# Sixteen rows of a grouped store, issued between the two halves of the last w2 load of an expert MLP

## The chip, the cores and the metric

The kernel runs on one core of one Trainium2 chip. The metric is the device time of one execution in microseconds. The times given are the median of several runs; the profile is of one execution, with its own time.

## The reference: what is computed

Eight experts, each with 256 rows of 512 numbers, go through two matrix products of their own with a ReLU between them. All inputs and the output are float32.

```
h   = max(matmul(x, w1) + b1, 0)       # x 8x256x512, w1 8x512x2048
out = matmul(h, w2) + b2               # w2 8x2048x512, out 8x256x512
```

The weights are 4 MB each, w1 and w2 for every expert: 64 MB of the 71.39 MB that the profile counts as read from HBM. The output is 4.19 MB.

## The kernel before

**Tiling.** TensorE works in float16. The weights come in by DMA on GpSimd's queue, which turns float32 into float16 on the way, so that a w1 or a w2 (4 MB in HBM) is 2 MB in SBUF. For one expert, `first_product` makes the hidden values in 16 pieces of 128 (each of four matmuls over the 512 inputs); ScalarE adds b1, applies ReLU and writes hT. `second_product` adds up b2 (one matmul with a row of ones) and 16 matmuls for each of two blocks of 128 output rows, in two PSUM tiles, po0 and po1. VectorE copies the one (L156) and ScalarE the other (L157) to an SBUF tile, from where it is stored.

**Staging.** The main loop (L229) runs over steps s = 0 to 10: step s holds the first product of expert s and the second product of expert s - 3 (LAG is 3). In steps 8, 9 and 10 only second products are left, of experts 5, 6 and 7. There are three buffers for w1 and three for w2.

**The ring.** The loads and some stores are issued on one queue, GpSimd's (POOL), in an order that the list `ring` fixes (L217 to L227): each entry has the step from which it is due, a function and its arguments, and at each step the loop takes entries from the head as long as they are due. An entry that isn't due holds up those behind it. `ordered` keeps the issue order of a queue as it stands in the program. A DMA that must wait (for a buffer to be free, or for the values that it stores) holds the queue. Entries at the end of the list: w2 of expert 6, w2 of expert 7, the store of experts 0 to 3, the store of experts 4 and 5.

**Halves.** The w2 of experts 6 and 7 is loaded as two DMAs of 1 MB in SBUF (`HALVED`, L91 to L93), and the second product of these experts first takes what reads the first half, for both output blocks, and then what reads the second (L175 to L178).

**Stores.** The results of experts 0 to 3 are gathered in one SBUF tile of 128 rows: expert e has rows 32e to 32e + 31, and each row holds eight output rows of 512 float32, 16 KB. They are stored together, 2 MB, by `flush` (L138 to L140) on GpSimd's queue. Experts 4 and 5 are gathered likewise, 64 rows each with 8 KB in a row, 1 MB. The tiles of experts 6 and 7 have 4 KB in each of 128 rows and are stored at once (L164): that of expert 6 in three parts (`PARTS`, L40), rows 0 to 24 and 121 to 127 by SyncE's queue and rows 25 to 120 by ScalarE's; that of expert 7 in one part by SyncE's queue.

Of the kernel before, what the change touches and what calls it, by code (L numbers as in the profile page):

```python
# [10 lines left out]
def kernel(  # L11
# [9 lines left out]
    nc = tc.nc  # L21
    fp32 = mybir.dt.float32
    fp16 = mybir.dt.float16
    E, T, H = x.shape
    M = w1.shape[2]
    P = 128
    nTB = T // P
    nKC = H // P
    nJ = M // P
    B = 32  # L30
    nB = P // B
    LAG = 3
# [6 lines left out]

    PARTS = {E - 2: ((0, 25, False), (25, 121, True), (121, 128, False))}  # L40
    nXF32 = 2
    X_LOADS = {2: 2, 4: 4}

    def ordered(ins):
        return tc.keep_in_program_order(ins)
# [3 lines left out]
    w2_pool = ctx.enter_context(tc.tile_pool(name="w2", bufs=3))  # L49
# [16 lines left out]
    w2_sb = [None] * E  # L66
    hT = [None] * E
    pending = {}
# [16 lines left out]
            out=w1_sb[e], in_=w1[e].rearrange("(p kc) m -> p kc m", kc=nKC)  # L85
        ))

    def load_w2(e):
        src = w2[e].rearrange("(p j) h -> p j h", j=nJ)
        w2_sb[e] = w2_pool.tile([P, nJ, H], fp16, tag="w2", name="w2sb")  # L90
        half = nJ // 2 if e in HALVED else nJ  # L91
        for lo in range(0, nJ, half):
            ordered(nc.gpsimd.dma_start(out=w2_sb[e][:, lo : lo + half], in_=src[:, lo : lo + half]))  # L93

    def transposes(e):
# [39 lines left out]
            if j == nJ // 2 and e + 1 < E:  # L135
                transposes(e + 1)

    def flush(first):  # L138
        dst, src = pending.pop(first)
        ordered(nc.gpsimd.dma_start(out=dst, in_=src))  # L140

    def store(e, po):
        if e in group_of:
# [48 lines left out]
    for e in range(nXF32):  # L192
# [4 lines left out]
        out=b2_sb,  # L197
        in_=b2.rearrange("e h -> (e h)").rearrange("(o f) -> o f", o=1),
# [10 lines left out]
    for b in range(nB):  # L209
        nc.vector.transpose(  # L210
            out=b1T[b * B : (b + 1) * B, nB - 1 - b : nB - 1 - b + nJ * B],
            in_=b1_rows.rearrange("r (i j) -> r j i", j=nJ),
# [4 lines left out]
    ring = []  # L217
    for s in range(1, E + LAG - 1):
        if s < E:
            if s in X_LOADS:  # L220
                ring.append((s - 2, load_x, (s, X_LOADS[s])))
            ring.append((s - 2, load_w1, (s,)))
        if s >= LAG:
            ring.append((s - 2, load_w2, (s - LAG,)))
    ring.append((E + LAG - 3, load_w2, (E - 1,)))
    for first, n in GROUPS.items():
        ring.append((first + n + LAG, flush, (first,)))  # L227

    for s in range(E + LAG):  # L229
        while ring and ring[0][0] <= s:  # L230
# [37 lines left out]
```

## Time and profile before

| what | value |
|---|---|
| median of 3 runs | 181.62 us (181.58 to 181.81) |
| time of the profiled execution | 181.49 us |
| its span, first to last instruction | 179.7 us |
| TensorE matmul busy | 130.7 us, 73% of the span |
| VectorE, ScalarE busy | 87.4 us, 71.0 us |
| GpSimd's DMA queue | 3200 packets, 38.28 MB |
| SyncE's, ScalarE's DMA queue | 1.70 MB, 0.46 MB |
| granted TensorE clock, mean | 0.919 of full speed |

How to read it: "span" runs from the first to the last instruction in the profile, and the execution's own time is a little more. The busy time of TensorE is a sum over matmuls that overlap. A DMA is cut into packets, which sixteen DMA engines carry; the queue of an issuing engine has its own stream on each of them. The DMA share of a stretch is the mean busy share of the sixteen engines (a little over 1 is possible, since packets overlap slightly), and GB/s counts bytes as they are written, so a weight load counts half of what it reads. [...]

### The profile page before, as it was taken

What the parts mean: (1) busy time and instruction counts of PE and PEld (TensorE: products, weight loads), DVE (VectorE), ACT (ScalarE), POOL (GpSimd) and SP (SyncE); (2) the same over time, 40 slices, a digit from 0 to 9 for tenths busy, and PEclk for the clock granted to TensorE, in tenths of its full rate; (3) what the DMA queues carried; (4) which work ended last, traced back from release to release, by engine and by line L of the source; (5) the groups of instructions that cost most, each with busy time, mean ns of one, the idle gap of its engine ahead of it and who ended that gap; (6) DMA issues with size and microseconds to landing.
All of it is one profiled execution on the core that took longest, in us unless ns stands there. A gap on an engine that the chain in (4) does not pass through costs nothing.

```text
span 179.7 us, 1958 instructions
## 1 busy us (share of the span) xinstructions
PE 130.7 (73%) x784; PEld 87.4 (49%) x784; DVE 87.4 (49%) x125; ACT 71.0 (40%) x152; POOL 12.5 (7%) x27
## 2 busy tenths in 40 slices
PE   0005999159895970999769994959499986999960
PEld 0004899149793320794359543934189432434420
DVE  0999938990000199999998699203200020301010
ACT  3001699318793022491267406930559020020010
POOL 6000030200201010001100001000200021010000
PEclk9999999858999696599988999999969997899998
DMA  5999999999998999999999999999999999999995
GB/s 208 274 197 213 233 204 208 230 224 193 228 233 184 224 233 219 193 230 230 193 219 233 212 197 233 230 193 219 233 208 201 233 212 202 217 215 213 344 422 239
DMA packets 3844, 40.56 MB, mean 226 GB/s; under 512 B 460, under 2 KB 476, under 8 KB 1148
## 3 DMA queue, kind: packets, MB, share of 16 engines
q0 software_dynamic: 3200, 38.28, 96.4%
q1 hardware_dynamic: 476, 1.70, 2.5%
q10 hardware_dynamic: 160, 0.46, 0.6%
q8 instruction: 6, 0.10, 0.2%
q14 instruction: 2, 0.02, 0.0%
HBM read 71.39 MB, written 4.19 MB: 421 GB/s over the span
## 4 chain that ended last, share of the span: by engine, by line
DMA 67%; PE 27%; POOL 1%; issue 1%; ACT 0%; another core or an unknown queue 0%; POOLq 0%
DMA w1sb<-in_w_dram 44%; DMA w2sb<-in_w_dram 23%; PE po L178 17%; PE ph L121 10%; PE po L171 1%; POOL w1sb L84 1%; ACT out L157 0%; POOL b_sb L196 0%; POOL x L76 0%; POOLq L252 0%
## 5 line engine op out<-in xcount | busy, mean ns | idle before, releaser
L121 PE MATMUL ph<-xT,w1sb 128*128 128x256 f16 x512 | 66.7, 299 | 36.2 <-DMA w1sb<-in_w_dram 30.0
L121 PEld LDWEIGHTS <-w1sb 128*128 128x128 f16 x512 | 60.9, 148 | 42.7 <-DMA w1sb<-in_w_dram 38.6
L128 ACT ACTIVATE hT<-ph,b1T 128x256 f16<-128x256 f32 x128 | 56.7, 475 | 36.9 <-PE ph L121 22.1
L112 DVE STREAM_TRANSPOSE xT<-x 32x256 f16<-32x256 f16 (+1 forms) x64 | 52.7, 885 | 28.0 <-DMA x<-in_x_dram 22.0
L178 PE MATMUL po<-w2sb,hT 128*128 128x512 f16 x256 | 59.9, 395 | 6.6 <-DMA w2sb<-in_w_dram 6.5
L178 PEld LDWEIGHTS <-hT 128*128 128x128 f16 x256 | 25.7, 101 | 40.7 <-issue 14.4
L156 DVE COPY out<-po 32x512 f32<-32x512 f32 (+2 forms) x22 | 15.1, 688 | 52.5 <-PE po L178 52.2
L157 ACT COPY out<-po 32x512 f32<-32x512 f32 (+2 forms) x22 | 12.7, 578 | 65.5 <-PE po L178 65.3
L109 DVE STREAM_TRANSPOSE xT<-x 32x256 f16<-32x256 f16 x32 | 14.0, 436 | 0.5
L93 POOL DMA_DIRECT2D w2sb<-in_w_dram x10 | 5.3, 535 | 73.9 <-PE po L178 73.9
L84 POOL DMA_DIRECT2D w1sb<-in_w_dram x8 | 4.5, 559 | 62.7 <-PE ph L121 61.9
L171 PE MATMUL po<-b_sb,ones 1*128 1x512 f16 x16 | 4.8, 379 | 0.0
L210 DVE STREAM_TRANSPOSE b1T<-b_rows 32x512 f32<-32x512 f32 x4 | 4.1, 1028 | 0.0
L203 DVE CAST x<-x 128x1024 f16<-128x1024 f32 x2 | 1.4, 694 | 3.3 <-DMA x<-in_x_dram 3.3
L171 PEld LDWEIGHTS <-ones 1*128 1x128 f16 x16 | 0.9, 92 | 2.1 <-issue 2.1
L140 POOL DMA_DIRECT2D out_dram<-out x2 | 1.1, 540 | 11.1 <-ACT out L157 11.1
L189 ACT ACT_TABLE_LOAD x1 | 1.3, 1283 | 0.7 <-PEq L252 0.7
L76 POOL DMA_DIRECT2D x<-in_x_dram x2 | 1.1, 557 | 0.0
L188 DVE MEMSET ones<- 1x128 f16 x1 | 0.2, 165 | 0.8 <-PEq L252 0.8
L196 POOL DMA_DIRECT2D b_sb<-in_b_dram x1 | 0.5, 507 | 0.0
L189 ACT ACTIVATE warm<-ones 1x128 f16<-1x128 f16 x1 | 0.3, 308 | 0.0
L252 POOL MEMSET const-float32-0.0<- 128x1 f32 x1 | 0.1, 98 | 0.2 <-issue 0.2
(3 smaller groups left out, 0.3 us busy)
## 6 DMA issues: line engine op xcount, KB each, us to landing
w1sb<-in_w_dram POOLq DMA_DIRECT2D x8, 2048.0 KB, 37.0
w2sb<-in_w_dram POOLq DMA_DIRECT2D x6, 2048.0 KB, 49.7
w2sb<-in_w_dram POOLq DMA_DIRECT2D x4, 1024.0 KB, 24.0
out_dram<-out POOLq DMA_DIRECT2D x1, 2048.0 KB, 26.7
x<-in_x_dram SPq DMA_DIRECT2D x2, 512.0 KB, 4.0
x<-in_x_dram POOLq DMA_DIRECT2D x1, 1024.0 KB, 35.6
out_dram<-out POOLq DMA_DIRECT2D x1, 1024.0 KB, 17.7
x<-in_x_dram POOLq DMA_DIRECT2D x1, 512.0 KB, 24.5
```

The lines of the kernel that those rows point to most:

```text
L84: ordered(nc.gpsimd.dma_start(out=w1_sb[e], in_=w1[e].rearrange("(p kc) m -> p kc m", kc=nKC)))
L93: ordered(nc.gpsimd.dma_start(out=w2_sb[e][:, lo : lo + half], in_=src[:, lo : lo + half]))
L109: nc.vector.transpose(out=out[:, :, g, :, 0, :], in_=block[:, :, :, 0, :])
L112: nc.vector.transpose(out=out[:, tb, g], in_=block[:, tb])
L121: ordered(nc.tensor.matmul(out=ph, lhsT=w1_sb[e][:, kc, :].rearrange("p (q j) -> p q j", j=nJ)[:, :, j], rhs=xT[e][:, kc, :], start=(kc == 0),
L128: nc.scalar.activation(out=hT[e][:, j, :].rearrange("p (tb k i) -> p tb k i", tb=nTB, k=split), in_=ph.rearrange("p (tb i k) -> p tb k i", ...
L156: nc.vector.tensor_copy(out=out_sb[at : at + rows, k * nTB, :], in_=po[0][part])
L157: nc.scalar.copy(out=out_sb[at : at + rows, k * nTB + 1, :], in_=po[1][part])
L171: ordered(nc.tensor.matmul(out=t, lhsT=ones1, rhs=b2_sb[0:1, e * H : (e + 1) * H], start=True, stop=False,))
L178: ordered(nc.tensor.matmul(out=po[tb], lhsT=hT[e][:, j, tb * P : (tb + 1) * P], rhs=w2_sb[e][:, j, :], start=False, stop=(j == nJ - 1),))
L189: ordered(nc.scalar.activation(out=warm, in_=ones1, func=mybir.ActivationFunctionType.Relu))
L210: nc.vector.transpose(out=b1T[b * B : (b + 1) * B, nB - 1 - b : nB - 1 - b + nJ * B], in_=b1_rows.rearrange("r (i j) -> r j i", j=nJ),)
```

## The change

In the last entry pair of the ring, the first 16 of the 128 rows of the grouped store of experts 0 to 3 (256 KB of 2 MB) are issued between the first and the second half of the load of expert 7's w2. The other 112 rows are stored where all 128 were. For this `load_w2` takes a list of the parts that it issues, and `flush` a range of rows; the store keeps its entry until its last row is issued.

```diff
+    EARLY = 16
...
-    def load_w2(e):
+    def load_w2(e, parts=(0, 1)):
         src = w2[e].rearrange("(p j) h -> p j h", j=nJ)
-        w2_sb[e] = w2_pool.tile([P, nJ, H], fp16, tag="w2", name="w2sb")
+        if 0 in parts:
+            w2_sb[e] = w2_pool.tile([P, nJ, H], fp16, tag="w2", name="w2sb")
         half = nJ // 2 if e in HALVED else nJ
         for lo in range(0, nJ, half):
+            if lo // half not in parts:
+                continue
             ordered(nc.gpsimd.dma_start(out=w2_sb[e][:, lo : lo + half], in_=src[:, lo : lo + half]))
...
-    def flush(first):
-        dst, src = pending.pop(first)
-        ordered(nc.gpsimd.dma_start(out=dst, in_=src))
+    def flush(first, p0=0, p1=P):
+        dst, src = pending[first]
+        ordered(nc.gpsimd.dma_start(out=dst[p0:p1], in_=src[p0:p1]))
+        if p1 == P:
+            del pending[first]
...
-    ring.append((E + LAG - 3, load_w2, (E - 1,)))
+    ring.append((E + LAG - 3, load_w2, (E - 1, (0,))))
+    ring.append((E + LAG - 3, flush, (0, 0, EARLY)))
+    ring.append((E + LAG - 3, load_w2, (E - 1, (1,))))
     for first, n in GROUPS.items():
-        ring.append((first + n + LAG, flush, (first,)))
+        ring.append((first + n + LAG, flush, (first, EARLY if first == 0 else 0)))
```

GpSimd issues one DMA more than before. The instructions of the other engines, and the DMAs of SyncE's and ScalarE's queues, are the same and in the same order.

## The prediction

> **What bounds the kernel now.** I read four views, in this order: the forty slices of the page, the chain that ended last, the stretches of the tail, and the group of instructions that touch w2sb in the tail.
>
> The slices come first, because the page's chain gives 67% to DMA.
>
> ```profile
> PE   0005999159895970999769994959499986999960
> ...
> DMA  5999999999998999999999999999999999999995
> GB/s 208 274 197 213 233 204 208 230 224 193 228 233 184 224 233 219 193 230 230 193 219 233 212 197 233 230 193 219 233 208 201 233 212 202 217 215 213 344 422 239
> ```
>
> The sixteen DMA engines never rest between the first slice and the last; TensorE rests often. The rate doubles in the last three slices, and not because the engines work harder: a weight is read as four bytes and written as two, a result is written as four. So the end is the sum of the DMA work, unless the tail has a hole in it. The chain of waits says something else about the tail:
>
> ```profile
> 108.47 41.12 DMA w2sb<-in_w_dram
> 149.59 0.04 issue
> 149.63 8.75 PE po L178 x32
> 158.39 0.53 PE po L171 x2
> 158.92 7.01 PE po L178 x32
> 165.93 0.53 PE po L171 x2
> 166.47 7.03 PE po L178 x32
> 173.49 0.02 issue
> 173.52 0.59 ACT out L157
> ```
>
> By it, three second products run back to back after the w2 of expert 5 lands, then the copy, then (not in the chain) the store of expert 7. Two things might therefore set the end: these products, or the queues. The stretches decide:
>
> ```profile
> core 0: us, PE busy (x) PEld busy (x) DVE busy (x) ACT busy (x) POOL busy (x), PEclk, DMA share, GB/s
> 149.60:159.30 9.70, 9.66 (x37) 3.74 (x37) 1.38 (x2) 0.86 (x2) 0.00 (x0) 0.82 1.04 216
> 159.30:167.40 8.10, 8.10 (x38) 3.45 (x37) 0.69 (x1) 0.88 (x2) 0.54 (x1) 1.00 1.03 212
> 167.40:175.00 7.60, 6.08 (x29) 2.55 (x26) 0.69 (x1) 0.59 (x1) 0.00 (x0) 1.00 0.99 407
> 175.00:177.60 2.60, 0.00 (x0) 0.00 (x0) 0.00 (x0) 0.00 (x0) 0.00 (x0) 1.00 0.94 391
> 177.60:179.70 2.10, 0.00 (x0) 0.00 (x0) 0.00 (x0) 0.00 (x0) 0.00 (x0) 0.61 0.19 78
> ```
>
> DMA stays at 0.94 or more until 177.6 us, where loads give way to stores at 167.4 (212 to 407 GB/s). TensorE's last product ends at 173.5 inside a full stretch. **The queues set the end**, with the products close behind.
>
> The trace's list of DMA packets (queue, start, length, bytes) refines this. The sixteen engines finish unevenly: five write their last packet at 177.1 to 177.4, one at 177.9, ten at 178.15 to 178.46. On the late ones the store of expert 7 starts only as the store of experts 4 and 5 ends (176.7 to 177.2), with no gap, though issued at 174.13 and under way on the early engines at 175.84.
>
> **The change, part by part.** The profiled execution took 181.49 us: span 179.7 and 1.79 around it. The median of the runs is 181.62, so 0.13 is added at the end.
>
> *What is moved.* The store of experts 0 to 3 has 2048 KB in 128 rows of 16 KB. Sixteen rows are 256 KB, at 407 GB/s 0.64 us. They go ahead of the last half load of w2; bytes are neither added nor removed. The half lands later by that, the other 112 rows as before: on an engine 0.64 earlier in one place is 0.64 later in another. I expect nothing from this by itself, since a full queue in another order ends at the same time.
>
> *Is TensorE held up?* The half was issued at 147.8 and lands 21.4 later:
>
> ```profile
> L178 PE MATMUL po<-w2sb,hT x128: 376/379/631, 139.9 to 173.1; 128*128 128x512 f16 x128
> L93 POOL DMA_DIRECT2D w2sb<-in_w_dram x2: 527/531/535, 147.3 to 147.8; - x2
> ...
> DMA to landing us min/median/max: 16.9/19.1/21.4
> ```
>
> So it lands at 169.2. The product of expert 7 starts at 166.47 and takes 7.03 for 32 matmuls, 0.22 each; the first that reads the second half is the 17th, at 166.47 + 16 x 0.22 = 170.0. The slack is 0.8 us (0.7 by the start of that matmul's record, 169.86). With 0.64 and the small terms below, 0.0 to 0.15 is left. If the cover is gone, the store of expert 7 is issued later by the stall; the late engines would not notice before the stall passes 176.9 - 175.84, about 1.1 us, because they still have the store of experts 4 and 5 to write. Price: zero.
>
> *One more issue on POOL.* Such an issue takes 0.53 (2 x 0.53 at 147.26). Queued behind it are the last half load and the two stores, which are issued 0.53 later, at 148.3 and on. The queue does not reach that half until about 163, some 14 us later; POOL itself then waits 11.1 us for the copies of expert 5. The new issue waits for the copies of expert 3, over well before 147, as the old one did. SP and ACT issue what they did. Price zero; 0.53 if the queue were empty.
>
> *One more completion on each engine.* In the list of packets a completion takes 0.022 among the loads. Plus 0.02.
>
> *Two more changes between loading and storing.* Before, the engines change once, at 167.5. Around it 40 of the load packets, mostly 0.625 elsewhere, take 0.678 (25, from 166) and 0.644 (15, from 167) on average: 25 x 0.053 + 15 x 0.019 = 1.6 us over 16 engines, 0.1 each. The change adds one more change of this kind and one back to loading, which no row shows. The nearest row for the way back is the first packets of x at the start, 0.61 where the rest take 0.16: at most 0.45. It cannot be below nothing, for a load packet is never shorter than 0.624. I take 0.1 for the pair, because the change that is seen costs that; ends 0 and 0.55.
>
> *Which engine gets which rows, and from where.* 16 rows give one to each engine (the b2 load, 16 pieces, shows 16 packets of 512 bytes), 112 give seven: eight in all, as before. But the sixteen rows are neighbours in SBUF, and the remainder no longer starts at row 0. If engines disturb each other there, packets stretch. The rows that speak to it are the three parts of expert 6's store, 25, 96 and 7 rows, read beside the big store: of the 96 packets on ACT's queue 95 take 0.159 and one 0.312, of 128 row packets of the big store 112 take 0.611 and 16 take 0.624. I take zero, by these rows. The upper end, from the farthest row (0.61 for 0.16, 3.8 times): the early packet takes 2.3 in place of 0.61, plus 1.7; if the other seven rows were each doubled, as the one packet was, a further 4.3.
>
> [...]
>
> Sum: 0.02 + 0.1 on 181.49, and 0.13 to the median: **181.74**, rounded to 181.7. A difference under 0.2% (0.36 us, from 181.26 to 181.98) is about what a measurement of this kernel can't tell from no change.
>
> **The rivals.**
>
> *A, the forecast:* same work, another order; 181.5 to 182.1, from nothing to the upper half of the cost of the changes.
>
> *B1, the early rows crowd (slower):* sixteen engines read from sixteen neighbouring rows at once, between the halves, and their packets stretch. No engine has idle time later, so any stretch on a late engine appears one for one at the end; it decides from 0.25 us on, where A's 0.12 and it pass 0.36. Doubled: +0.6, so 182.35; at 3.8 times: +1.7, so 183.4. For it: rows this close together have no row in the trace. Against it: 95 of 96 packets.
>
> *B2, the remainder crowds too (slower):* the 112 rows are cut in sevens from row 16, so engines meet at the same part of SBUF again and again. One to four of seven doubled: +0.6 to +2.4 beside B1, so 183 to 186. For it: it would act on 1.75 MB, not on 0.25. Against it: the 96 rows in sixes from row 25, unhurt.
>
> *C, the ends even out (faster):* the five early engines idle for 1.06 us at the end. If another division of rows evened the ends, the gain is at most 5 x 1.06 / 16 = 0.33 us, 181.3. Against it: one and seven are eight on each engine.
>
> *D, TensorE stalls:* the slack is overrun. With B1's stretch by up to 1.7 the stall is up to 1.7, of which 1.1 is covered; alone 0.5 of stall gives 181.7 still; 1.7 gives 182.3.
>
> **How the numbers follow.** A 0.44 (0.42 of it within 0.2%, 0.02 slower), B1 0.22, B2 0.15, D 0.07 (0.04 within, 0.03 slower), C and unforeseen gains 0.12 (0.08 faster, 0.04 within). Faster 0.08, same 0.50, slower 0.42. The range takes A, B1, D and most of C: from 181.3 to 183.4; above it lies most of B2, below it part of C, under 2 in 10.
>
> **What would show it.** In the profile after: the last half lands about 0.65 to 0.75 later than 169.2; the 17th matmul of expert 7 shows no wait, or one under 0.1; the DMA share stays at 0.94 or more up to 177.6 and the last packets end at 178.4 to 178.6. Sixteen packets of 16384 bytes stand between the halves, 0.61 to 0.62 each; longer ones mean B1. The 112 others longer than 0.63 mean B2. A stretch below 0.9 in DMA share anywhere after 160, or an engine set that ends more evenly, would make the forecast wrong.

## The result

| | median | runs | ratio to before |
|---|---|---|---|
| before | 181.69 us | 6, 181.45 to 181.81 | |
| after | 183.24 us | 6, 182.65 to 184.85 | 1.0091 (1.0064 to 1.0118) |

The change costs 1.55 us, 0.9%, and the runs after it scatter over 2.2 us where those before scatter over 0.4. The profiled execution after took 182.65 us with a span of 180.8, 1.1 longer than before. So the profile shows the mildest of these runs, and the time that it lost is less than the median's. Ratios, here and below, go by fast runs alone; of the split in place below one run, 187.6 us, is counted as slow, being over 1.5% above that kernel's fastest.

### The profile page after: what moved, and what is told of

Its sections match the earlier page's. It is cut to its first block, busy times and chain, and to the rows that moved or that the text cites. A ratio compares the mean times of both kernels' runs of the same rounds, so it can differ in the third digit from the quotient of the medians.

```text
span 180.8 us, 1960 instructions
## 1 busy us (share of the span) xinstructions
PE 130.2 (72%) x784; PEld 86.4 (48%) x784; DVE 87.3 (48%) x125; ACT 70.8 (39%) x152; POOL 13.1 (7%) x28
## 4 chain that ended last, share of the span: by engine, by line
DMA 55%; PE 24%; another core or an unknown queue 8%; issue 5%; POOL 2%; ACT 2%; POOLq 0%
DMA w1sb<-in_w_dram 43%; PE ph L125 13%; DMA w2sb<-in_w_dram 12%; PE po L184 11%; ACT out L163 2%; POOL w2sb L97 1%; POOL w1sb L85 1%; PE po L177 1%; POOL b_sb L202 0%; POOL x L77 0%; ACT hT L132 0%; POOL out_dram L144 0%; POOLq L144 0%; POOLq L97 0%
## 5 line engine op out<-in xcount | busy, mean ns | idle before, releaser
L125 PE MATMUL ph<-xT,w1sb 128*128 128x256 f16 x512 | 64.8, 293 | 33.8 <-DMA w1sb<-in_w_dram 27.1
L125 PEld LDWEIGHTS <-w1sb 128*128 128x128 f16 x512 | 59.7, 147 | 39.7 <-DMA w1sb<-in_w_dram 35.8
L184 PE MATMUL po<-w2sb,hT 128*128 128x512 f16 x256 | 61.4, 401 | 9.6 <-DMA w2sb<-in_w_dram 9.6
L144 POOL DMA_DIRECT2D out_dram<-out x3 | 1.6, 537 | 10.2 <-ACT out L163 10.2
```

The lines of the kernel that those rows point to most:

```text
L125: ordered(nc.tensor.matmul(out=ph, lhsT=w1_sb[e][:, kc, :].rearrange("p (q j) -> p q j", j=nJ)[:, :, j], rhs=xT[e][:, kc, :], start=(kc == 0),
L144: ordered(nc.gpsimd.dma_start(out=dst[p0:p1], in_=src[p0:p1]))
L184: ordered(nc.tensor.matmul(out=po[tb], lhsT=hT[e][:, j, tb * P : (tb + 1) * P], rhs=w2_sb[e][:, j, :], start=False, stop=(j == nJ - 1),))
```

## The profile after

TensorE, DMA and rate by slices, from the page of the kernel after:

```profile
PE   0006989169995950999779696969495969999940
...
DMA  6999999999999999999999999999999999999995
GB/s 217 262 210 198 232 221 196 221 234 217 194 232 201 227 214 225 225 207 207 232 214 203 221 232 207 207 225 228 210 207 225 225 194 212 216 226 234 354 342 223
```

DMA is as full as before. What fell is the rate in the last full slice, where only stores are left, from 422 GB/s to 342: busy engines, fewer bytes. The same stretches as in the prediction, of the kernel after (columns as there; the last three are the granted clock, the DMA share and GB/s):

```profile
159.30:167.40 8.10, 8.10 (x38) 3.42 (x37) 0.69 (x1) 0.64 (x2) 0.56 (x1) 1.00 1.03 228
167.40:175.00 7.60, 5.99 (x28) 2.44 (x25) 0.69 (x1) 0.59 (x1) 0.00 (x0) 1.00 0.99 349
175.00:177.60 2.60, 0.00 (x0) 0.00 (x0) 0.00 (x0) 0.00 (x0) 0.00 (x0) 0.78 0.98 397
177.60:179.70 2.10, 0.00 (x0) 0.00 (x0) 0.00 (x0) 0.00 (x0) 0.00 (x0) 0.50 0.54 220
```

From 159.3 to 167.4 the rate is higher by 16 GB/s: the early 256 KB are in it, and nothing is lost there. From 167.4 to 175.0 it is 349 in place of 407. Part of that is right, since the last half load ends later and counts half; the rest is the loss. From 177.6 on the engines still work at 0.54 where they had all but ended at 0.19.

The last half load and the wait for it, from the instructions that touch w2sb and from the order of time:

```profile
L97 POOL DMA_DIRECT2D w2sb<-in_w_dram x2: 530/544/559, 147.3 to 148.3; - x2
...
DMA to landing us min/median/max: 16.9/19.3/21.6
```

```profile
166.15 3.63 PE L184 MATMUL po<-w2sb,hT 128*128 128x512 f16 x16
...
170.04 3.61 PE L184 MATMUL po<-w2sb,hT 128*128 128x512 f16 x16 [0.26 <-DMA w2sb<-in_w_dram]
```

The half lands at 148.35 + 21.65 = 170.0, by the chain of waits, 0.8 later than before, and TensorE waits 0.26 us for it; its product had also begun 0.25 earlier than before, at 166.15 in place of 166.40. The store of expert 7 is then issued only 0.2 later than before. That is not where 1.1 us went.

The trace's list of DMA packets shows where. Row packets of the big store last 0.61 to 0.62 when nothing disturbs them; "long" means over 0.63 us. The last column is the start of the last packet of all.

```
kernel   early 16 KB packets   the other 16 KB packets   4 KB packets of experts 6, 7   last packet
before   -                     128, none long            256, 1 over 0.18               178.46
after    16, none long         112, 17 long, to 1.26     256, 13 over 0.18              179.62
```

The long packets begin at 169.6 and go on to 175. In sum the 16 KB packets last 6.4 us too long, the 4 KB packets 4.1, the 8 KB packets of the loads and of experts 4 and 5 some 3.9 more than before: 14 us over 16 engines, 0.9 on each, of the 1.16 by which the last packet is later. The loss stands in the tail of stores, on the 112 rows and on what runs beside them; 0.08 of the 0.9 is on the last loads.

## The experiments

Three theories. **T**: the remainder of 112 rows, cut among the engines from row 16 on, makes them disturb each other. **U**: a store between two loads is what costs. **V**: the 16 neighbouring rows crowd. Later T splits into **S** (they meet in SBUF) and **H** (in HBM). Each comparison is with before, run on the same chip, 181.48 to 181.57 us.

```
run                                      median    ratio to before (95%)    long 16 KB packets
split in place (16 + 112)                186.48    1.022 (1.017 to 1.027)   33 of 128
columns moved                            181.75    1.001 (1.000 to 1.002)   (14 and 4 KB; none long)
rows 64 + 64, in place                   185.52    1.022 (1.021 to 1.024)   59 of 128
early copy, remainder whole              182.16    1.004 (1.002 to 1.005)   0 of 144
halves of SBUF, spread in HBM            186.95    1.030 (1.024 to 1.035)   58 of 128
all of SBUF, halves of HBM               181.66    1.000 (0.999 to 1.001)   (8 KB; none long)
even and odd rows                        181.71    1.001 (1.000 to 1.002)   0 of 128
16 rows in place, then all 128           183.35    1.010 (1.008 to 1.011)   19 of 144
112 rows alone                           183.31    1.009 (1.006 to 1.012)   22 of 112
16 spread rows in place, then all 128    182.42    1.005 (1.004 to 1.007)   3 of 144
```

The split in place has four runs, from 184.75 to 187.6: by their median it lies 5.0 us above before, by its ratio 3.9 (3.0 to 4.8).

**The split without the move.** In `flush` of before:

```diff
-        ordered(nc.gpsimd.dma_start(out=dst, in_=src))
+        for p0, p1 in ((0, 16), (16, P)) if first == 0 else ((0, P),):
+            ordered(nc.gpsimd.dma_start(out=dst[p0:p1], in_=src[p0:p1]))
```

> Rows 0 to 15 and rows 16 to 127 of the grouped store are two DMAs, but both stand where the one stood, after the last w2 load; nothing is moved. Theory T (the 112 rows, cut in sevens from row 16, make engines disturb each other): the loss stays, 1.0 to 1.8 us above before, about 183, and stretched 16384-byte packets are seen among the 112. Theory U (a store between two loads costs, whatever rows it has): the time of before, 181.7, no stretched packets. Theory V (the 16 neighbouring rows crowd): packets of the 16 stretch, the 112 do not, some 0.5 us above before.

Its tail by stretches:

```profile
167.40:175.00 7.60, 4.66 (x21) 1.85 (x19) 0.69 (x1) 0.59 (x1) 0.00 (x0) 1.00 1.02 350
175.00:177.60 2.60, 0.00 (x0) 0.00 (x0) 0.00 (x0) 0.00 (x0) 0.00 (x0) 0.72 0.93 342
177.60:179.70 2.10, 0.00 (x0) 0.00 (x0) 0.00 (x0) 0.00 (x0) 0.00 (x0) 0.50 0.70 267
179.70:182.00 2.30, 0.00 (x0) 0.00 (x0) 0.00 (x0) 0.00 (x0) 0.00 (x0) 0.50 0.15 61
```

Engines fully busy at 350 GB/s, where before moved 407: stretched packets, no hole. U can't explain it, for nothing was moved. But T missed the size: 3.9 to 5.0 us in place of 1.0 to 1.8. The split in place is worse than the change. Two of the 16 packets that come first are long here too, up to 1.65 us, which V had said; a run below takes this up.

**The move without the split of rows.** As after, but `flush` cuts columns:

```diff
-    EARLY = 16
+    EARLY = 1
...
-    def flush(first, p0=0, p1=P):
+    def flush(first, r0=0, r1=None):
         dst, src = pending[first]
-        ordered(nc.gpsimd.dma_start(out=dst[p0:p1], in_=src[p0:p1]))
-        if p1 == P:
+        ordered(nc.gpsimd.dma_start(out=dst[:, r0:r1], in_=src[:, r0:r1]))
+        if r1 is None:
             del pending[first]
```

> The same 256 KB are moved to the same place, but as the first 2 KB of each of the 128 rows; the remainder is 14 KB of each of the 128 rows. Theory T: both DMAs have 128 rows, as before, so the loss goes: 181.6 to 181.9. Theory U: the move is what costs, so 183.2 stays. Theory V: 181.6 to 181.9, as T.

181.75: the same bytes in the same place in the queue cost at most 0.2%, and U falls. This is what the forecast priced. It gains nothing either, as the full queue in another order ended when it did: the last packet starts at 178.48, before at 178.46.

**Halves of 64 rows.** The first diff with `((0, 64), (64, P))`.

> The grouped store is cut into rows 0 to 63 and rows 64 to 127, both in the old place. [...] Theory T with HBM's side as the place (uneven pieces of seven rows): pieces of four rows are even, so 181.7 to 182.2. Theory U: 181.7.

```profile
167.40:175.00 7.60, 4.64 (x21) 1.85 (x19) 0.69 (x1) 0.59 (x1) 0.00 (x0) 1.00 1.05 334
175.00:177.60 2.60, 0.00 (x0) 0.00 (x0) 0.00 (x0) 0.00 (x0) 0.00 (x0) 0.67 0.85 246
177.60:179.70 2.10, 0.00 (x0) 0.00 (x0) 0.00 (x0) 0.00 (x0) 0.00 (x0) 0.50 0.91 367
```

4.0 us above before, though the pieces are even: uneven pieces are not what it takes, and the 181.7 to 182.2 for the HBM side and U's 181.7 are both out. Nearly half of the packets are long, 59 of 128.

**The early rows with the remainder whole.** As after, but the 16 rows go to expert 7's place in the output, which its own store overwrites, and the 128 rows follow whole:

```diff
         dst, src = pending[first]
-        ordered(nc.gpsimd.dma_start(out=dst[p0:p1], in_=src[p0:p1]))
-        if p1 == P:
-            del pending[first]
+        if p1 < P:
+            dst = out[E - 1].rearrange("(p r) h -> p r h", r=2 * group_of[first][1])
+            ordered(nc.gpsimd.dma_start(out=dst[p0:p1], in_=src[p0:p1]))
+            return
+        ordered(nc.gpsimd.dma_start(out=dst, in_=src))
+        del pending[first]
...
-        ring.append((first + n + LAG, flush, (first, EARLY if first == 0 else 0)))
+        ring.append((first + n + LAG, flush, (first, 0)))
```

> The early DMA of 16 rows stays between the two halves, but writes the rows to the place of expert 7's output, which the store of expert 7 overwrites later; all 128 rows of the grouped store then follow in one DMA, as before. So 256 KB are written twice, 0.64 us more work on each engine. Theory T: only these 0.64 us are added, 182.2 to 182.5, and no packet of the 128 rows is stretched. Theories U and V: the loss of 1.2 to 1.6 us comes on top, 183.5 to 184.

```profile
167.40:175.00 7.60, 4.57 (x21) 1.78 (x19) 0.69 (x1) 0.59 (x1) 0.00 (x0) 1.00 1.01 396
175.00:177.60 2.60, 0.00 (x0) 0.00 (x0) 0.00 (x0) 0.00 (x0) 0.00 (x0) 1.00 0.97 408
```

182.16, 0.64 above before (0.4 to 0.9 by the ratio): the time of the 256 KB that are written twice. The 16 rows among the loads are free of loss, and 128 rows behind them as well. V falls for the change as it stands, and what remains is the 112 rows.

**SBUF or HBM.** Two runs that take the sides apart; in both the output rows of experts 0 to 3 stand in another order. The first reads SBUF as the 64 and 64 rows did, and spreads the writes:

```diff
+        if first == 0:
+            dst = dst.rearrange("(p i) r h -> i p r h", i=2)
+            for i in range(2):
+                ordered(nc.gpsimd.dma_start(out=dst[i], in_=src[i * 64 : (i + 1) * 64]))
+            return
```

> The grouped store in two DMAs of SBUF rows 0 to 63 and 64 to 127, as the run with 64 and 64 rows had it, but each is written to every second 16 KB row of all 2 MB in HBM (so the output rows of experts 0 to 3 stand in another order). Theory S (engines meet on the SBUF side, by the rows that a DMA reads): 185 to 186, as with 64 and 64. Theory H (they meet on the HBM side, because each DMA writes one dense megabyte): 181.6 to 182.

The second reads all rows and writes a dense megabyte each:

```diff
+        if first == 0:
+            halves = dst.rearrange("(i p) r h -> i p r h", i=2)
+            whole = src.rearrange("p (i r) h -> i p r h", i=2)
+            for i in range(2):
+                ordered(nc.gpsimd.dma_start(
+                    out=halves[i].rearrange("p (k r) h -> (p k) r h", k=2), in_=whole[i]))
+            return
```

> The reverse: each of two DMAs reads half of the columns (8 KB) of all 128 rows in SBUF and writes one dense megabyte in HBM (the output of experts 0 to 3 stands in another order). Theory S: 181.6 to 182. Theory H: 185 to 186.

186.95 and 181.66: for the halves S holds and H falls. Their loss goes with the rows that are read in SBUF and not with where they are written. The two sides were not taken apart for the 112 rows; that theirs is the same is an inference. The 186.95 is 1.4 above the 64 and 64 rows; spreading the writes did not help, and whether it hurt is open.

**Even and odd rows.** Two DMAs of 64 rows again, `dst[i::2]` from `src[i::2]`.

> The grouped store in two DMAs, of the 64 even rows and the 64 odd rows, in the old place. Each DMA reaches rows all over SBUF. Theory S, if only the rows that a DMA reaches in all count: 181.6 to 182. Theory S, if it counts which rows the engines read at the same time (four neighbours in every second row each, two engines beside each other at any time): 182.5 to 185.

```profile
167.40:175.00 7.60, 4.56 (x21) 1.78 (x19) 0.69 (x1) 0.58 (x1) 0.00 (x0) 1.00 1.00 411
175.00:177.60 2.60, 0.00 (x0) 0.00 (x0) 0.00 (x0) 0.00 (x0) 0.00 (x0) 0.58 0.91 381
177.60:179.70 2.10, 0.00 (x0) 0.00 (x0) 0.00 (x0) 0.00 (x0) 0.00 (x0) 0.50 0.18 74
```

411 GB/s and no long packet. So neither the number of DMAs nor 64 rows in one of them costs, only 64 neighbours (185.52). Of the two readings of S the first, that only the rows reached in all count, came true here, and the price of the second did not. But the first does not explain the change: its 112 rows leave out only one eighth of the rows of SBUF. What it is about them that stretches packets, their seven for each engine or their start at row 16, no run tells.

The stores of 128 rows here, in parts of 2, 8, 14 and 16 KB of a row, showed no long packet by themselves: none before, none with the early copy, none with the columns and none with the halves of HBM. The trace does not name the engine of a packet, so which engine takes which of the 112 rows no run here shows.

**The 16 rows beside other stores.** The early copy again, but issued after the last load:

```diff
-    ring.append((E + LAG - 3, load_w2, (E - 1, (0,))))
+    ring.append((E + LAG - 3, load_w2, (E - 1,)))
     ring.append((E + LAG - 3, flush, (0, 0, EARLY)))
-    ring.append((E + LAG - 3, load_w2, (E - 1, (1,))))
```

> After the last w2 load come first the 16 rows, written to expert 7's place (overwritten later), then all 128 rows in one DMA; 256 KB are written twice. If only the remainder's 112 rows cost, it is 0.64 us above before, 182.1 to 182.4, as with the early copy. If the 16 neighbouring rows cost too as soon as other reads of SBUF come right behind them, which would explain why the split in place lost more than the change itself, it is 183 to 185.

183.35 less 181.57 is 1.78: 0.64 for the bytes and 1.14 for crowding. The same DMA costs 0.64 among loads and 1.78 among stores. This explains a part of why the split in place lost more than the change. Stores read SBUF and loads write it; whether that is the reason was not tried apart.

**Sixteen spread rows.** The same, with `src[p0::8]`.

> As the run with the 16 rows in place and the remainder whole, but the 16 rows are every eighth row of SBUF in place of 16 neighbours. Theory S, by how many engines meet at one part of SBUF: spread rows meet less, 182.1 to 182.6 in place of 183.35. If only the number of rows in the DMA counts: 183.2 to 183.5 again.

182.42 less 181.48 is 0.94, of which 0.30 is crowding, where neighbours cost 1.14; 3 packets are long in place of 19. The number of rows in the DMA is the same.

**The 112 rows alone.** In `flush` of before, the first 16 rows are not stored at all:

```diff
+        lo = 16 if first == 0 else 0
+        ordered(nc.gpsimd.dma_start(out=dst[lo:], in_=src[lo:]))
```

> Only rows 16 to 127 of the grouped store are stored, in the old place; the first 16 rows are left out (256 KB of the output are not written), 0.64 us less work on each engine. If the 112 rows, cut in sevens from row 16, are the whole loss of the change (1.55 us), the time is 181.57 - 0.64 + 1.55 = 182.5, 182.2 to 183, with stretched packets among the 112. If the loss needs the early rows, 180.9 to 181.1.

183.31, though 256 KB less are written:

```profile
167.40:175.00 7.60, 4.70 (x22) 1.85 (x19) 0.69 (x1) 0.58 (x1) 0.00 (x0) 1.00 1.02 360
175.00:177.60 2.60, 0.00 (x0) 0.00 (x0) 0.00 (x0) 0.00 (x0) 0.00 (x0) 1.00 0.91 366
177.60:179.70 2.10, 0.00 (x0) 0.00 (x0) 0.00 (x0) 0.00 (x0) 0.00 (x0) 0.69 0.39 160
```

Engines are busy at 1.02 and move 360 GB/s. The 112 rows in the old place cost 183.31 - 181.48 + 0.64 = 2.5 us; the early rows are not needed for the loss. That is more than the 1.55 of the change and more than was expected; the run's own scatter is 1.5 us. With the 1.1 of the 16 rows it is 3.6, and the split in place lost 3.9 (3.0 to 4.8) by its ratio and 5.0 by its median. Whether anything is left over, by each making the other worse, is open.

## Why the prediction went as it did

The forecast, A, 181.7, was wrong by 1.5 us, and what happened is its rival B2. That 183.24 lies inside the range, 181.3 to 183.4, is luck: the upper end was put there for B1, which did not happen, and most of B2 was said to lie above it.

*What bounds the kernel:* right. The DMA engines were busy to the end, at 0.98 or more in each stretch up to 177.6 us, and the stretches of packets, 0.9 us on each engine, are most of the 1.16 by which the last packet came later.

*What is moved:* right. The same bytes in the same place as columns cost at most 0.2%.

*Is TensorE held up:* the price of zero was right, the cover was not. The half landed 0.8 later where 0.65 to 0.75 was taken, and the stall was 0.26 in place of at most 0.1. The cover of 0.8 us belonged to the one profiled execution, where the granted clock was 0.82 from 149.6 to 159.3. With the even and odd rows, at a clock of 1.00 there, the last product began at 164.72 and TensorE waited 0.99 us for the half, and the time was that of before. With the early copy it waited 1.96 us, and only the bytes were paid.

*Issue, completion, changes between loading and storing:* right as far as seen. The loads from 157 to 170 us last, over 0.625 each, 0.20 too long on each engine after, 0.12 before: 0.08 where 0.1 was taken for the pair.

*Which engine gets which rows, and from where:* this is the step that failed. It took zero "by these rows", the 0.159 us packets of the 25, 96 and 7 rows; the runs showed 1.55 us, with 17 of the 112 packets long. Those DMAs have rows of 4 KB, 0.5 MB in all, beside a store of 128 rows; the 112 rows have 1.75 MB. 95 undisturbed packets of a small DMA were no bound for a large one; why they were undisturbed was not tried. For the early 16 rows the runs show no loss among loads and 1.14 us among stores; the loss of the change came from the 112.

*B1 and B2:* B1 said that the early packets stretch. They did not, 16 of 16 lasted 0.624. B2 said that the remainder crowds, 183 to 186 together with B1; without B1 its own +0.6 to +2.4 gives 182.3 to 184.1, and 183.24 lies in it. Its sum was not what happened, though: 17 of 112 is about one in seven, but by 0.4 us on each engine and not 0.6, and another 0.5 came on the packets of loads and other stores, which it had not priced. The observation that spoke against B2, the 96 rows in sixes, was weighed too high; B2 had 0.15.

## What to carry to other kernels

Where the queues set the end, try to cut a store by columns of all rows or by every second row, not by a block of rows: here the same 2 MB in two DMAs took 181.7 us by columns or by even and odd rows, and 185.5 by upper and lower half. A split that moves a small piece must be priced for what it does to the remainder: here the moved 16 rows were free and the 112 left behind cost the whole. A DMA share near 1 does not say that the engines move what they could: from 167.4 to 175.0 us the even and odd rows moved 411 GB/s at 1.00, the 112 rows alone 360 at 1.02. Read it with GB/s, and where the trace has them with the lengths of single packets.

## What the runs showed of the hardware that I had not expected

The same 16-row store costs its bytes alone among loads (0.64 us) and 1.78 us among stores. The long packets of the larger parts do not begin with the store: in the halves of 64 rows the first 34 or so, from 167.5 to 169.6, last 0.61 to 0.62 each, and the long ones follow, up to 2.46 us; of the 112 rows after the change the first 30 are short, from 168.2 to 169.6. The 16 rows issued among stores have long ones at once, from 167.6. No run shows why. And in the kernels with the 112 rows the time is uncertain: before scattered over 0.4 us, the change over 2.2, the split in place over 2.9, the 112 rows alone over 1.5. The halves of 64 rows, with the most long packets, scattered over 0.4 only; with their writes spread, over 2.2.
